# Latent gates merged in one bank per feature tile, and score masks issued behind all of a head's products

## The chip, the cores and the metric

The kernel runs on one core of a Trainium2 chip. The metric is the device time of one execution in microseconds (us), the median over repeated executions. The profile is one such execution, recorded by the hardware; all times are in us from its first instruction unless marked ns.

## The reference

Two networks run one after the other on one sequence of 256 tokens with 2048 features, all in float32. The first has four layers, of three kinds; the change touches two of the kinds.

```python
# layers 0 and 3: differential attention, 8 heads, two score maps a head
sc = einsum('bqhcd,bkhcd->bhcqk', q[:, s:e], k[:, :e]) * scale
sc = where(chunk_mask(s, e - s, e), sc, -inf)
pr = softmax(sc)
w = pr[:, :, 0] - lam * pr[:, :, 1]
# layer 1: latent attention, 16 heads
c_q, c_kv, k_pe, gate = split(xn @ w_in, ...)
sc = (einsum('bqhd,bkhd->bhqk', q_nope, k_nope) + einsum('bqhr,bkr->bhqk', q_pe, k_pe)) * scale
sc = where(chunk_mask(s, e - s, e), sc, -inf)
y = einsum('bhqk,bkhe->bqhe', softmax(sc), v) * silu(gate)
```

A query sees all keys of its own 64-token chunk and of those before it. Queries are taken 128 at a time, the first block with 128 keys, the second with 256. Layer 2 is a gated linear recurrence. After each of the four a gated projection of a side input is added. The second network has one state-space layer and one dilated attention layer. Neither is touched by the change.

## The kernel before

**Products in three parts.** Float32 weights and activations are each split into a high part and a rest, and a product is hi·hi + hi·lo + lo·hi. `chunks` (L307) walks over the feature blocks of 128 (k), loads the weights on SyncE's queue 1 MB at a time (`load`, L285: three buffers), and splits them (`split`, L291) 1024 columns at a time: the high part by ScalarE (L300), the rest by VectorE (L302), three buffers each. After each block it calls `ktick`, and after each chunk `chunk_tick`.

**Order of work.** TensorE's order is mostly the program's. The main line is the large projections. Everything else of a head (norms, rotations, scores, softmax, weighted sums) is written as a job, a generator that yields a number of ticks to wait; `ktick` (L261) steps jobs whose wait is over, so their instructions fall between the products of a projection. Loads and splits get a higher priority, 150 instructions ahead. A planner orders each engine's instructions by priority and by readiness and gives out the buffers.

**Two forms of the product with features on partitions.** `matB` (L326) issues three products of 256 columns for each block and feature tile: hi with the activations' high part, hi with their rest, lo with their high part (L335), all into the same 256 columns of a PSUM bank. `matM` (L349) is the merged form: hi with high part and rest side by side, 512 columns (L357), then lo with the high part, 256 columns (L358); the two halves of the result are added afterwards by `join` (L361): ScalarE copies one half out (L364) and VectorE adds it to the other (L365). `matA` (L374, products on L385) has tokens on partitions.

**Differential attention** (`layer_a`, L782). For each of four groups of two heads the key, query, gate and value projections run, then two `head` jobs (L851). A head (L855 to L881) takes for each of the two query blocks t and each of the two maps c a float32 score product (L861; TensorE runs a float32 product as two instructions), then a mask product in bfloat16 (L864): a matrix whose first row is minus a large number for the first 64 queries, times ones, 64 columns wide. VectorE takes the maximum (L867), GpSimd scales it (L869), ScalarE takes exponentials and sums (L873). After a wait come the transposes (L888 to L890), and later the weighted sum (L895 to L897).

**Latent attention** (`layer_b`, L967). First the latents (`latents`, L1030, by `matM`), then the 64 shared key features. Then gates and head pairs alternate, eight of each (L1211): `gate(q)` (L1182) projects 256 features of the output gate by `matB` into one bank, multiplies by the token norm (L1189) and applies SiLU (L1191); `heads(m)` (L1204) projects queries and keys and values of two heads by `matA` and starts the jobs `uq` (L1066; squares on L1074, transposes L1062 and L1097), `ukv` (L1100; squares L1112, scaled keys L1051, transposes L1062, copied out by L1064) and, 11 ticks later, `pair` (L1123). So the jobs of pair m run within the gate that follows it, and the rest of `pair` (the scaling L1156, the transposes L1164, the sums L1173 to L1178) within the next projections. `pair` takes for each query block two float32 products over 128 features (L1133), two over the 64 rotated features (L1137, on half the rows of the array each) and two masks (L1140).

**PSUM.** Small results share four banks (`ps`, L241); the large accumulators have two of two banks each.

Of the kernel before, what the change touches and what calls it, by code (L numbers as in the profile page):

```python
# [13 lines left out]
BF16 = mybir.dt.bfloat16  # L14
# [4 lines left out]
P = 128  # L19
T = 256  # L20
# [29 lines left out]
for _n, _c in _ROW_SPEC:  # L50
# [6 lines left out]
    "a_w_out": (16, [512] * 4, None),  # L57
    "b_w_in": (16, [256] * 4 + [64] + [256] * 8, None),
    "b_w_uq": (4, [384] * 8, None),
# [129 lines left out]
class Build:  # L189
# [116 lines left out]

    def chunks(self, W, kts, n0, n, merged=False):  # L307

# [4 lines left out]
        for k0, k1 in zip(cuts[:-1], cuts[1:]):  # L313
            src = W.part(n0, n, k0, k1)
            with self.tc.high_priority(offset=self.ahead):
                if self.early:
                    self.early.pop(0)()
                w = self.load(src, k1 - k0, n)
                parts = self.split(w, k1 - k0, n)
            for k in range(k0, k1):  # L320
                yield k, parts[k - k0]
                if not merged or k % 2:
                    self.ktick()
            self.chunk_tick()
# [24 lines left out]
    def matM(self, W, kts, n0, x):  # L349

        a = self.pa.tile([P, 2, 512], F32, name="acc", tag="acc")
        for k, (hi, lo) in self.chunks(W, kts, n0, 256, True):
            xh, _ = x(k)
# [148 lines left out]
    def setup(self):  # L502
# [34 lines left out]
        nc.vector.memset(self.mask[0:1, 0:64], -BIG)  # L537
        self.ones16 = cp.tile([P, 64], BF16, name="ones16")
        nc.vector.memset(self.ones16, 1.0)
# [242 lines left out]
    def layer_a(self, layer, j, x, acc, prep):  # L782
# [68 lines left out]
        def head(h, pend, w1, w2):  # L851
            g, c0 = h // 2, 2 * (h % 2)
            self.finish(*pend)
            vs = slice(T * (h % 2), T * (h % 2) + T)
            ws = []  # L855
            for t in range(2):
                nk = (t + 1) * P
                sc = self.ps()
                scv = sc[:, :2 * nk].rearrange("p (c k) -> p c k", c=2)
                for c in range(2):  # L860
                    nc.tensor.matmul(  # L861
                        out=scv[:, c, :], lhsT=Q[g][:, c0 + c, t * P:(t + 1) * P], rhs=K[g][:, c0 + c, :nk],
                        start=True, stop=False)
                    nc.tensor.matmul(  # L864
                        out=scv[:, c, nk - 64:], lhsT=self.mask, rhs=self.ones16, start=False, stop=True)
                mx = self.small([P, 2])
# [100 lines left out]
    def layer_b(self, layer, x, acc, prep):  # L967
# [155 lines left out]
        def pair(m):  # L1123
# [6 lines left out]
            for t, o0, nk in spans:  # L1130
                qs = slice(t * P, (t + 1) * P)
                for i in range(2):
                    nc.tensor.matmul(  # L1133
                        out=scs[i][:, o0:o0 + nk], lhsT=QT[g][:, c + i, qs], rhs=KT[g][:, c + i, :nk], start=True, stop=False)
                for i in range(2):
                    pr = slice(64 * i, 64 * i + 64)
                    nc.tensor.matmul(  # L1137
                        out=scs[i][:, o0:o0 + nk], lhsT=QPv[pr, qs], rhs=st["kpe"][pr, :nk], start=False, stop=False)
                for i in range(2):
                    nc.tensor.matmul(  # L1140
                        out=scs[i][:, o0 + nk - 64:o0 + nk], lhsT=self.mask, rhs=self.ones16, start=False, stop=True)
            mx, nm, sm, rs = (self.small([P, 2, 2]) for _ in range(4))
# [39 lines left out]
        def gate(q):  # L1182

            a = self.ps()
            self.matB(W, 16, 1088 + 256 * q, 256, x, [(a[:, :T], True, False), (a[:, T:], False, True)])
            if q % 2 == 0:
                sg[q // 2] = self.slot()
            t = sg[q // 2][:, 2 * (q % 2):2 * (q % 2) + 2, :]
            nc.vector.tensor_tensor(  # L1189
                out=t, in0=a.rearrange("p (a b) -> p a b", a=2), in1=nst["rb"].unsqueeze(1).to_broadcast([P, 2, T]), op=ALU.mult)  # L1190
            nc.scalar.activation(t, t, AF.Silu)  # L1191

# [802 lines left out]
```

## Time and profile before

| | |
|---|---|
| median of 3 runs | 3326.06 us (3325.78 to 3326.6) |
| the profiled execution | 3327.28 us |
| its span, first to last instruction | 3325.5 us |
| TensorE, busy | 3281.4 us |
| weight loads, busy (beside products) | 2778.0 us |
| VectorE, busy | 2349.4 us |
| ScalarE, busy | 1876.1 us |
| GpSimd, busy | 282.3 us |
| HBM | 206 GB/s over the span |
| granted TensorE clock, mean | 0.995 of full speed |

PE is TensorE's products, PEld its weight loads, DVE VectorE, ACT ScalarE, POOL GpSimd, SP SyncE. A row of the order of time gives start, duration, engine, line, operation, out<-in with shapes, the count of instructions that it merges and, in brackets, the idle time before it and what ended it. Products overlap: the duration of one runs well past the start of the next, so what a product costs is read from starts. `ps` and `acc` are tiles in PSUM, `t` is a temporary, `s` a large slot, `w` raw weights, `hi` and `lo` their split parts.

### The profile page before, as it was taken

Reading aid. Unit: us, or ns where it says so; the run is one execution under the profiler, and the core shown is the slowest. Engines: PE = TensorE matmul, PEld = TensorE weight load, DVE = VectorE, ACT = ScalarE, POOL = GpSimd, SP = SyncE. Lnnn points to the kernel's source line nnn. Section 1 sums busy time; section 2 is a strip of 40 time slices with the busy share of each in tenths; the row PEclk is TensorE's granted clock in tenths of the full one; section 3 lists DMA queues with packets and bytes.
Section 4 is the critical chain, followed back from the end, with each engine's and each line's share of the span. In section 5 each row is a group of like instructions: output and inputs, shape, how many; then the busy total and the mean of one; then the engine's idle time right before and its main releaser. Section 6 shows DMA issues by size and latency. Waiting matters only on the chain. (4 is left out here: it accounts for less than half of the span.)

```text
span 3325.5 us, 45091 instructions
## 1 busy us (share of the span) xinstructions
PE 3281.4 (99%) x17244; PEld 2778.0 (84%) x17244; DVE 2349.4 (71%) x3217; ACT 1876.1 (56%) x2668; POOL 282.3 (8%) x551
## 2 busy tenths in 40 slices
PE   8999999999999999999999999999999999999997
PEld 7888888898888888888888888888888887888887
DVE  8766766666667886776676677777777767787567
ACT  5555545566655776555555554568777545444454
POOL 3111200122100000001112000000000000000002
PEclk9999999999999999999999999999999999999999
DMA  7656666544466545666566565554555666876442
GB/s 276 231 203 222 214 221 225 195 143 143 149 237 222 196 178 196 230 230 223 201 217 213 197 234 204 184 201 166 190 184 184 235 236 238 299 296 240 161 143 102
DMA packets 114345, 686.65 MB, mean 206 GB/s; under 512 B 13328, under 2 KB 14032, under 8 KB 47696
## 3 DMA queue, kind: packets, MB, share of 16 engines
q1 hardware_dynamic: 109152, 670.49, 56.9%
q10 hardware_dynamic: 4976, 13.27, 1.4%
q8 instruction: 135, 2.21, 0.3%
q14 instruction: 82, 0.67, 0.1%
HBM read 681.55 MB, written 2.16 MB: 206 GB/s over the span
## 5 line engine op out<-in xcount | busy, mean ns | idle before, releaser
L300 ACT ACTIVATE hi<-w 128x1024 fp32r<-128x1024 f32 x1082 | 1141.9, 1056 | 1224.0 <-PE acc L385 747.7
L302 DVE TENSOR_TENSOR lo<-w,hi 128x1024 fp32r<-128x1024 f32 x1082 | 1322.0, 1224 | 671.1 <-ACT hi L300 656.5
L357 PE MATMUL acc<-x,hi 128*128 128x512 f32 x2816 | 1003.6, 400 | 2.2 <-ACT t L364 1.5
L385 PE MATMUL acc<-hi,x 128*128 128x512 f32 x2688 | 844.5, 394 | 4.6 <-ACT hi L300 3.2
L385 PE MATMUL acc<-hi,s 128*128 128x512 f32 (+1 forms) x2560 | 791.0, 390 | 2.5 <-DVE t L1085 2.5
L358 PE MATMUL acc<-x,lo 128*128 128x256 f32 x2816 | 790.6, 281 | 0.0
L357 PEld LDWEIGHTS acc<-x,hi 128*128 128x128 f32 x2816 | 528.7, 188 | 130.7 <-issue 5.3
L385 PEld LDWEIGHTS acc<-hi,x 128*128 128x128 f32 x2688 | 502.6, 189 | 109.3 <-ACT hi L300 3.4
L385 PEld LDWEIGHTS acc<-hi,s 128*128 128x128 f32 x2560 | 474.6, 188 | 94.1 <-issue 2.7
L358 PEld LDWEIGHTS acc<-x,lo 128*128 128x128 f32 x2816 | 531.9, 189 | 3.0 <-issue 2.4
L385 PE MATMUL acc<-lo,x 128*128 128x512 f32 x1344 | 527.1, 392 | 5.5 <-DVE lo L302 5.5
L385 PE MATMUL acc<-lo,s 128*128 128x512 f32 (+1 forms) x1280 | 495.7, 387 | 1.7 <-DVE lo L302 1.7
L385 PEld LDWEIGHTS acc<-lo,x 128*128 128x128 f32 x1344 | 253.6, 189 | 60.2 <-DVE lo L302 6.4
L385 PEld LDWEIGHTS acc<-lo,s 128*128 128x128 f32 x1280 | 240.3, 188 | 50.6 <-DVE lo L302 2.9
L1381 DVE SCALAR_TENSOR_TENSOR aacc<-aw,siluc,aacc 128x512 f32<-128x512 f32 x255 | 190.9, 749 | 68.8 <-DMA aw<-in_ada_w_dram 66.0
L335 PE MATMUL ps<-x,hi 128*128 128x256 f32 (+1 forms) x576 | 108.2, 286 | 0.0
L463 POOL TENSOR_TENSOR m<-m,mhalf 128x4 f32<-128x4 f32 (+2 forms) x61 | 80.0, 1311 | 173.1 <-DVE m L1794 164.5
L335 PEld LDWEIGHTS ps<-x,hi 128*128 128x128 f32 (+1 forms) x576 | 88.6, 185 | 1.2 <-DVE x L733 0.2
L1381 DVE SCALAR_TENSOR_TENSOR ssacc<-s,siluc,ssacc 128x512 f32<-128x512 f32 x105 | 78.6, 748 | 9.7 <-DMA s<-in_ada_w_dram 8.5
L1245 DVE SCALAR_TENSOR_TENSOR s<-s,vecs 128x254 f32<-128x254 f32 (+2 forms) x192 | 80.8, 477 | 1.5 <-ACT s L1243 1.3
L335 PE MATMUL ps<-x,lo 128*128 128x256 f32 (+1 forms) x288 | 81.2, 282 | 0.0
L470 POOL TENSOR_TENSOR m<-ss 128x4 f32<-128x4 f32 x7 | 3.2, 461 | 848.0 <-ACT t L695 848.0
(391 smaller groups left out, 2869.5 us busy)
## 6 DMA issues: line engine op xcount, KB each, us to landing
w<-in_a_w_in_dram SPq DMA_DIRECT2D x127, 1024.0 KB, 4.9
w<-in_a_in_w_dram SPq DMA_DIRECT2D x80, 1024.0 KB, 4.8
aw<-in_ada_w_dram SPq DMA_DIRECT2D x136, 512.0 KB, 4.1
w<-in_ple_w_gate_dram SPq DMA_DIRECT2D x64, 1024.0 KB, 5.2
w<-in_kv_w_dram SPq DMA_DIRECT2D x48, 1024.0 KB, 4.8
w<-in_a_w_out_dram SPq DMA_DIRECT2D x32, 1024.0 KB, 5.1
w<-in_c_w_in_dram SPq DMA_DIRECT2D x32, 1024.0 KB, 4.9
w<-in_a_out_w_dram SPq DMA_DIRECT2D x32, 1024.0 KB, 4.9
```

The lines of the kernel that those rows point to most:

```text
L300: nc.scalar.activation(hi[:, :m], src, AF.Copy)
L302: nc.vector.tensor_tensor(out=lo[:, :m], in0=src, in1=hi[:, :m].bitcast(F32), op=ALU.subtract)
L335: self.nc.tensor.matmul(out=o, lhsT=a[:, c0:c1], rhs=b, start=(k == 0 and p == 0 and first), stop=(k == kts - 1 and p == 2 and last))
L357: self.nc.tensor.matmul(out=a[:, i, :], lhsT=hi[:, c], rhs=xx, start=(k == 0), stop=False)
L358: self.nc.tensor.matmul(out=a[:, i, :T], lhsT=lo[:, c], rhs=xh, start=False, stop=(k == kts - 1))
L385: self.nc.tensor.matmul(out=outs[t][:, :n], lhsT=b[:, s], rhs=w, start=(k == 0 and p == 0), stop=(k == kts - 1 and p == 2))
L463: self.nc.gpsimd.tensor_tensor(out=out, in0=in_, in1=h, op=ALU.pow)
L470: self.nc.gpsimd.tensor_tensor(out=q, in0=acc[:, 0:2, :], in1=acc[:, 2:4, :], op=ALU.add)
L1245: nc.vector.scalar_tensor_tensor(out=dst[:, s:], in0=src[:, :T - s], scalar=self.vec(wname, (3 - s) * nct + ct), in1=dst[:, s:], op0=ALU.m ...
L1381: nc.vector.scalar_tensor_tensor(out=st["acc"], in0=w[:, i, :], scalar=c, in1=st["acc"], op0=ALU.mult, op1=ALU.add)
```

## The change

The gate projection takes one feature tile of 128 at a time, in the merged form of two products, each tile into a bank of `ps` of its own; ScalarE copies the second half of the bank out, VectorE adds it to the first half, and multiply and SiLU follow in SBUF once for both tiles. The weights of the gate columns are stored 128 wide for that, one chunk for each tile. `chunks` takes the number of blocks after which it ticks in place of the flag. In a differential head all score products are issued first, then one mask for each query block over both maps (2 x 64 columns). In a latent pair all products over 128 features come first, then those over 64, then one mask for each head over both query blocks. The first product in a bank alone carries the start flag.

```diff
--- before.py
+++ after.py
@@ -55,7 +55,7 @@
 _WEIGHTS = {
     "a_w_in": (16, [512] * 16, None),
     "a_w_out": (16, [512] * 4, None),
-    "b_w_in": (16, [256] * 4 + [64] + [256] * 8, None),
+    "b_w_in": (16, [256] * 4 + [64] + [128] * 16, None),
     "b_w_uq": (4, [384] * 8, None),
     "b_w_ukv": (4, [512] * 8, None),
     "b_w_out": (16, [512] * 4, None),
@@ -304,7 +304,7 @@
                 parts.append((hi[:, k * n:(k + 1) * n], lo[:, k * n:(k + 1) * n]))
         return parts
 
-    def chunks(self, W, kts, n0, n, merged=False):
+    def chunks(self, W, kts, n0, n, every=1):
 
         step = max(1, 2048 // n)
         cuts = list(range(0, kts, step)) + [kts]
@@ -319,7 +319,7 @@
                 parts = self.split(w, k1 - k0, n)
             for k in range(k0, k1):
                 yield k, parts[k - k0]
-                if not merged or k % 2:
+                if k % every == every - 1:
                     self.ktick()
             self.chunk_tick()
 
@@ -349,7 +349,7 @@
     def matM(self, W, kts, n0, x):
 
         a = self.pa.tile([P, 2, 512], F32, name="acc", tag="acc")
-        for k, (hi, lo) in self.chunks(W, kts, n0, 256, True):
+        for k, (hi, lo) in self.chunks(W, kts, n0, 256, 2):
             xh, _ = x(k)
             xx = x.pair(k)
             for i in range(2):
@@ -535,7 +535,7 @@
         self.mask = cp.tile([P, P], BF16, name="mask")
         nc.vector.memset(self.mask, 0.0)
         nc.vector.memset(self.mask[0:1, 0:64], -BIG)
-        self.ones16 = cp.tile([P, 64], BF16, name="ones16")
+        self.ones16 = cp.tile([P, 2, 64], BF16, name="ones16")
         nc.vector.memset(self.ones16, 1.0)
         self.pos = cp.tile([P, 2], F32, name="posf")
         self.posi = posi
@@ -852,17 +852,20 @@
             g, c0 = h // 2, 2 * (h % 2)
             self.finish(*pend)
             vs = slice(T * (h % 2), T * (h % 2) + T)
-            ws = []
+            ws, scs = [], []
             for t in range(2):
                 nk = (t + 1) * P
-                sc = self.ps()
-                scv = sc[:, :2 * nk].rearrange("p (c k) -> p c k", c=2)
+                scv = self.ps()[:, :2 * nk].rearrange("p (c k) -> p c k", c=2)
                 for c in range(2):
                     nc.tensor.matmul(
                         out=scv[:, c, :], lhsT=Q[g][:, c0 + c, t * P:(t + 1) * P], rhs=K[g][:, c0 + c, :nk],
-                        start=True, stop=False)
-                    nc.tensor.matmul(
-                        out=scv[:, c, nk - 64:], lhsT=self.mask, rhs=self.ones16, start=False, stop=True)
+                        start=(c == 0), stop=False)
+                scs.append(scv)
+            for t in range(2):
+                nk = (t + 1) * P
+                nc.tensor.matmul(out=scs[t][:, :, nk - 64:], lhsT=self.mask, rhs=self.ones16, start=False, stop=True)
+            for t in range(2):
+                nk, scv = (t + 1) * P, scs[t]
                 mx = self.small([P, 2])
                 nc.vector.tensor_reduce(out=mx, in_=scv, axis=AX.X, op=ALU.max)
                 nm = self.small([P, 2])
@@ -1131,14 +1134,18 @@
                 qs = slice(t * P, (t + 1) * P)
                 for i in range(2):
                     nc.tensor.matmul(
-                        out=scs[i][:, o0:o0 + nk], lhsT=QT[g][:, c + i, qs], rhs=KT[g][:, c + i, :nk], start=True, stop=False)
+                        out=scs[i][:, o0:o0 + nk], lhsT=QT[g][:, c + i, qs], rhs=KT[g][:, c + i, :nk],
+                        start=(t == 0), stop=False)
+            for t, o0, nk in spans:
+                qs = slice(t * P, (t + 1) * P)
                 for i in range(2):
                     pr = slice(64 * i, 64 * i + 64)
                     nc.tensor.matmul(
                         out=scs[i][:, o0:o0 + nk], lhsT=QPv[pr, qs], rhs=st["kpe"][pr, :nk], start=False, stop=False)
-                for i in range(2):
-                    nc.tensor.matmul(
-                        out=scs[i][:, o0 + nk - 64:o0 + nk], lhsT=self.mask, rhs=self.ones16, start=False, stop=True)
+            for i in range(2):
+                nc.tensor.matmul(
+                    out=scs[i].rearrange("p (a k) -> p a k", a=2)[:, :, 64:P], lhsT=self.mask, rhs=self.ones16,
+                    start=False, stop=True)
             mx, nm, sm, rs = (self.small([P, 2, 2]) for _ in range(4))
             es = [self.tmp(384), self.tmp(384)]
             for i in range(2):
@@ -1181,14 +1188,20 @@
 
         def gate(q):
 
-            a = self.ps()
-            self.matB(W, 16, 1088 + 256 * q, 256, x, [(a[:, :T], True, False), (a[:, T:], False, True)])
             if q % 2 == 0:
                 sg[q // 2] = self.slot()
-            t = sg[q // 2][:, 2 * (q % 2):2 * (q % 2) + 2, :]
-            nc.vector.tensor_tensor(
-                out=t, in0=a.rearrange("p (a b) -> p a b", a=2), in1=nst["rb"].unsqueeze(1).to_broadcast([P, 2, T]), op=ALU.mult)
-            nc.scalar.activation(t, t, AF.Silu)
+            v = sg[q // 2][:, 2 * (q % 2):2 * (q % 2) + 2, :]
+            for i in range(2):
+                a = self.ps()
+                for k, (hi, lo) in self.chunks(W, 16, 1088 + 256 * q + P * i, P, 2):
+                    xh, _ = x(k)
+                    nc.tensor.matmul(out=a, lhsT=hi, rhs=x.pair(k), start=(k == 0), stop=False)
+                    nc.tensor.matmul(out=a[:, :T], lhsT=lo, rhs=xh, start=False, stop=(k == 15))
+                u = self.tmp(T)
+                nc.scalar.activation(u, a[:, T:], AF.Copy)
+                nc.vector.tensor_tensor(out=v[:, i, :], in0=a[:, :T], in1=u, op=ALU.add)
+            nc.vector.tensor_tensor(out=v, in0=v, in1=nst["rb"].unsqueeze(1).to_broadcast([P, 2, T]), op=ALU.mult)
+            nc.scalar.activation(v, v, AF.Silu)
 
         def close(j):
             self.finish(pairs[2 * j], pairs[2 * j + 1])
```

## Rows read from the trace of the kernel before

**Rows 1.** The page's first part: TensorE's products, busy us, share, instructions.

```profile
PE 3281.4 (99%) x17244; PEld 2778.0 (84%) x17244; DVE 2349.4 (71%) x3217; ACT 1876.1 (56%) x2668; POOL 282.3 (8%) x551
```

**Rows 2.** Busy time by stretch: length, PE, PEld, DVE, ACT, POOL, clock, DMA, GB/s.

```profile
100.00:410.00 310.00, 309.83 (x1451) 256.02 (x1450) 213.02 (x281) 168.19 (x256) 54.63 (x123) 1.00 0.61 215
...
705.25:733.17 27.92, 27.77 (x193) 25.06 (x192) 17.73 (x38) 17.68 (x32) 7.16 (x16) 1.00 0.41 142
718.49:728.99 10.50, 10.50 (x67) 9.66 (x66) 7.33 (x15) 10.24 (x19) 0.20 (x1) 1.00 0.54 184
```

**Rows 3.** Order of time, TensorE, ten triples of a gate apart.

```profile
677.79 0.40 PE L335 MATMUL ps<-x,hi 128*128 128x256 f32 x2
...
681.39 0.40 PE L335 MATMUL ps<-x,hi 128*128 128x256 f32 x2
```

**Rows 4.** Order of time, TensorE, 18 merged pairs of the latents apart.

```profile
629.82 0.39 PE L357 MATMUL acc<-x,hi 128*128 128x512 f32 x1
...
636.06 0.39 PE L357 MATMUL acc<-x,hi 128*128 128x512 f32 x1
```

**Rows 5.** Order of time, VectorE, within one period of layer 1.

```profile
712.83 0.76 DVE L1051 TENSOR_TENSOR t<-acc,m 128x256 f32<-128x256 f32 x2 [1.97 <-POOL m L625]
713.50 2.08 DVE L302 TENSOR_TENSOR lo<-w,hi 128x1024 fp32r<-128x1024 f32 x2
...
721.49 0.69 DVE L1189 TENSOR_TENSOR s<-ps,rb 128x512 f32<-128x512 f32 x1 [1.16 <-PE ps L335]
...
725.69 0.55 DVE L1156 TENSOR_SCALAR t<-t,m 128x128 f32<-128x128 f32 x2
```

**Rows 6.** Groups of 650 to 870: count, busy us, mean ns, idle before.

```profile
L1112 ACT ACTIVATE t<-acc 128x256 f32<-128x256 f32 x14 | 5.4, 385 | 14.4 <-PE ps L335 13.5 <-DVE t L612 0.9
```

**Rows 7.** Waits of weight loads, 650 to 910: total us, times, longest.

```profile
PEld ps L1164 <- PE acc L385: 2.0, 8, 0.4
PEld ps L1062 <- issue: 1.9, 6, 0.3
```

**Rows 8.** Order of time, TensorE: the key heads' transposes.

```profile
713.40 0.68 PE L1062 MATMUL ps<-ident,t 128*128 128x128 f32 x4
```

**Rows 9.** Order of time, ScalarE: first and last of the full stretch.

```profile
718.49 0.84 ACT L300 ACTIVATE hi<-w 128x768 fp32r<-128x768 f32 x1 [3.68 <-PE ps L335]
...
728.06 0.87 ACT L1074 ACTIVATE t<-acc 128x384 f32<-128x384 f32 x2
```

**Rows 10.** Order of time, TensorE: scores and masks of a differential head.

```profile
112.49 0.38 PE L861 MATMUL ps<-s 128*128 128x128 f32 x2
112.71 0.19 PE L864 MATMUL ps<-ones,mask 128*128 128x64 bf16 x1
112.73 0.47 PE L861 MATMUL ps<-s 128*128 128x128 f32 x2
113.04 0.19 PE L864 MATMUL ps<-ones,mask 128*128 128x64 bf16 x1
...
114.15 0.71 PE L385 MATMUL acc<-hi,x 128*128 128x512 f32 x2
```

**Rows 11.** Order of time, TensorE: scores and masks of a latent pair.

```profile
686.94 0.71 PE L1133 MATMUL ps<-s 128*128 128x128 f32 x4
687.58 0.49 PE L1137 MATMUL ps<-s 64*128 64x128 f32 x4
688.01 0.23 PE L1140 MATMUL ps<-ones,mask 128*128 128x64 bf16 x2
688.07 1.11 PE L1133 MATMUL ps<-s 128*128 128x256 f32 x4
689.11 0.70 PE L1137 MATMUL ps<-s 64*128 64x256 f32 x4
689.75 0.23 PE L1140 MATMUL ps<-ones,mask 128*128 128x64 bf16 x2
689.82 0.37 PE L335 MATMUL ps<-x,hi 128*128 128x256 f32 x1
```

## The prediction

> **What bounds the kernel now.** I began with the busy shares. TensorE is busy for 99% of the span [rows 1], so only time on its own instruction stream can be saved, and an added instruction elsewhere matters only where TensorE ends up waiting for it. The profiled execution took 3327.28 us, its span is 3325.5, and the median of the three runs is 3326.06; the sum below is a difference and is taken off the median.
>
> Next came the busy time by stretch [rows 2]. In the first attention layer TensorE is busy for 309.83 of 310.00 us: nothing is waited for there, and what its stream loses the kernel gains. One period of the latent layer, a gate and a head pair's projections, is 27.92 us long, and seven of the eight gates are followed by one. The other engines look free in it, at 17.7 us each. But one stretch of 10.50 us within the period has ScalarE busy for 10.24. That is where the argument turns.
>
> Last I read the order of time of each engine around the three places that the diff edits [rows 3 to 11].
>
> **Gates, on TensorE.** A gate has 16 feature blocks times 2 halves. Each now takes three products of 256 columns; with the change it takes one of 512 and one of 256. The columns are equal, and one weight load and one start in three go. Ten such triples take 681.39 − 677.79 = 3.60 us, 0.360 each [rows 3]. The merged form already stands in this layer's latents: 18 pairs take 636.06 − 629.82 = 6.24 us, 0.3467 each [rows 4]. The difference is 0.0133 us, times 32 it is 0.43 us a gate, times 8 gates 3.4 us, if all of it reached the end.
>
> Weight transfers stay: one load of 1 MB per half replaces one of 1 MB per 8 blocks, 8 KB a partition both times, as many splits, and the background ticks come after the same number of columns. SyncE gets nothing new.
>
> **Gates, on the other engines.** One VectorE multiply out of PSUM of 512 columns (0.69 us, at 721.49 [rows 5]) becomes two ScalarE copies and two VectorE adds of 256 columns out of PSUM, and the same multiply within SBUF. The nearest ScalarE row is 385 ns, an instruction of the same shape out of PSUM [rows 6]; behind another it may cost less, so I take 0.28 to 0.385. The nearest VectorE row is 0.76 for two [rows 5], 0.38 each.
>
> **What the gates' gain meets.** In six of the eight gates TensorE waits 0.3 us ahead of the transposes of the key heads [rows 7]: their inputs are two VectorE instructions begun at 712.83 and together 0.76 long, and TensorE starts on the first of them at 713.40 [rows 5, 8]. VectorE itself had waited 1.97 us for GpSimd. That chain through ScalarE, VectorE and GpSimd begins where the row of 718.49 begins it for the next period: TensorE frees a buffer of split weights right behind the score products. From there ScalarE runs nearly without a gap up to the squares of the query projection at 728.06 [rows 2, 9], and everything after hangs on those. So the period is the length of this chain plus the score products, and TensorE's faster gates only lengthen its wait. Of the 32 triples only one or two, between the score products and the freed buffer, still shorten the period: 0.02 us.
>
> The copy of a gate's second half falls into that full ScalarE stretch (the multiply that follows the gate starts at 721.49 [rows 5]), so the chain grows by 0.28 or more. The copy of the first half is ready near 711.6 (the gate's start at 705.25 [rows 2], 16 pairs of 0.347 and six transposes at the 0.11 of a small product), where VectorE idles until 712.83 [rows 5]; I cost it at nothing. What hides it is that idle stretch, and if its order is bad it holds up the transposes by the add's 0.38.
>
> **Masks of the differential heads.** A head now issues eight score products, with a mask of 64 columns after every two. Two small products alone take 112.71 − 112.49 = 0.22 us; behind a mask they take 113.04 − 112.73 = 0.31 [rows 10]. A mask streams for 0.03 and is too short to cover the load of the next float32 weights: about 0.085 is exposed behind each of the four, the last one ahead of the next projection. With the change all eight products stand first, and two masks of 128 columns follow. Their columns are equal, three of four exposures go, and the last shrinks by the 0.03 that the longer mask covers, to 0.055. A head saves 4 × 0.085 − 0.055 = 0.28 us; 2 layers of 8 heads save 4.5 us.
>
> The first query tile's maximum now waits for the second tile's products: at 112.49 + 4 × 0.11 + 4 × 0.216 = 113.79 its mask starts, 0.75 later than the one at 113.04. VectorE's queue behind that maximum holds the next split of weights, and TensorE needs that only two or three buffers later, so I cost it at nothing. The second tile is 0.25 earlier, and the transposes wait for it. Bounds: 0.2 to 0.34 a head.
>
> **Masks of the latent pairs.** A pair takes 689.82 − 686.94 = 2.88 us from its first score product to the gate's next product [rows 11], and eight pairs run. By its rows: the change from 128-row to 64-row products costs about 0.09 (0.64 for four products of 0.11, of which 0.10 is the first weight load) and comes once instead of twice; the exposure behind the middle masks, 0.085, goes; four masks of 0.03 to 0.04 become two of 0.056, saving 0.02; the last exposure shrinks by 0.03. Sum 0.23 us a pair, 1.8 us in all.
>
> Four 64-row products over 128 columns take 688.01 − 687.58 = 0.43 us, two groups of 0.21, so about 0.10 a group is lost even between two groups of the same kind [rows 11]; I keep that loss. The Trainium skill's page "TensorEngine Tiling (Array Packing)", Key Properties, says that changing the tiling mode drains the engine and changing only the tile does not. By that the two groups that become neighbours would lose nothing, and a pair would save 0.33 instead of 0.23.
>
> **The sum.** Heads −4.5. The first gate, which meets no key chain, −0.4. The second, with most of its triples ahead of waits, −0.2. The first and the last pair, which lie outside the steady periods, −0.5. In each of seven periods −0.23 (pair) − 0.02 (triples) + 0.28 (copy) + 0.10 (the add and the longer chain on VectorE, taken low because only part of it stands in the way) = +0.13, so +0.9. Total −4.7 us, taken against 3326.06: 3321.4 us, and 3322.6 for a profiled execution like the one shown.
>
> About 0.2%, 6.65 us, is what a measurement of this kernel can tell from no change. The forecast lies inside it.
>
> **Rivals.** *The full gain.* If the order of ScalarE's queue comes out so that no copy stands in the chain, or the splits run further ahead because a chunk has fewer instructions, the terms are 3.4 + 4.5 + 1.8 = 9.7 us: 3316.4. For it: VectorE and ScalarE are free 10 us in each period [rows 2]. Against it: the six waits of 0.3 us, which stand before any copy is added. Chance 0.25.
>
> *The add and the multiply land before the softmax's last scaling.* VectorE scales the second head's weights at 725.69 [rows 5], and TensorE already waits in all eight pairs for its transposes [rows 7]. An add of 0.38 and a multiply of 0.69, less overlap, are 0.94 us in that queue; the periods then lose 0.94 − 0.25 = 0.69 each, 4.8 in all, and −5.6 + 4.8 = −0.8: 3325.3. It decides from about 0.8 us a period. Chance 0.13.
>
> *A bank is held (slower).* A gate now fills two banks of the four that it shares with the transposes and scores. If the first half's add stands behind the two splits of 713.50 (2.08 us [rows 5]) its bank comes free at 713.50 + 2.08 + 0.38 = 715.96, and a score product due one period after 686.94 [rows 11], at 714.86, waits 1.1 us. Over seven periods that is 7.7: 3329.1. Beyond 0.67 us a period the gain of 4.7 is gone. Against it: the key transposes' own bank is free again by then. Chance 0.08.
>
> *Masks over two separate runs stream slower.* Both new masks write two runs of 64 columns; no row shows such a product. If it took twice its 0.056, 48 masks would add 2.7 us: 3324.1. The Trainium skill's "PSUM — Partial Sum Buffer", Specifications (TRN2), warns that any non-contiguous access pattern slows matmuls significantly, by no stated figure; no row here bears that out. Chance 0.05.
>
> **How the numbers follow.** The forecast has 0.49. Faster by over 0.2% is the full gain and the forecast's good edge, 0.29. Slower by over 0.2% needs waits for a bank of 1.6 us a period, or two of the costs at once: 0.07. The rest, 0.64, is within. The range runs from the full gain with the heads at their upper bound (3.4 + 16 × 0.34 + 1.8 = 10.6: 3315.4) to the second rival with the masks' price on top (3325.3 + 2.7 = 3328.0), and leaves out the held bank.
>
> **What would show it.** In the changed profile a gate pair of products should start every 0.347 us; a head should span 1.41 us from its first product to the next projection instead of 1.66; a pair 2.68 instead of 2.88. The period should stay between 27.8 and 28.2 us, with the wait ahead of the key transposes grown to 0.5 us or more and ScalarE's stretch longer by one copy. The forecast is wrong if the period falls below 27.5 (the chain did not bind) or rises past 28.5 (another wait), or if heads span over 1.5 us.

## The result, and the profile after

The changed kernel takes 3345.33 us (median of 4 runs, 3344.52 to 3346.83) against 3326.33 for the kernel before; the ratio is 1.0055, with a 95% interval of 1.0043 to 1.0066. It is 19 us slower, and the prediction's range ended at 3328.0. The profiled execution took 3345.09 us, its span is 3343.0.

The page's first part, with the engines' busy time, answers to [rows 1]:

```profile
PE 3277.3 (98%) x16940; PEld 2761.5 (83%) x16940; DVE 2353.9 (70%) x3233; ACT 1880.9 (56%) x2684; POOL 274.7 (8%) x551
```

TensorE has 4.1 us less to do in 304 fewer instructions, VectorE and ScalarE have 4.5 and 4.8 us more. None of this is 19 us: nearly all of the time was lost in waits. The busy time by stretch answers to [rows 2] (same columns); the second line is one period of the latent layer, from a query projection to the next:

```profile
100.00:410.00 310.00, 309.73 (x1442) 255.81 (x1441) 214.39 (x284) 169.13 (x257) 55.72 (x123) 1.00 0.61 217
754.05:784.48 30.43, 27.46 (x161) 23.12 (x160) 18.56 (x39) 18.34 (x33) 6.49 (x15) 1.00 0.37 130
```

The first attention layer is as full as before. The period has grown from 27.92 to 30.43 us, and TensorE is idle for 2.97 us of it, at a granted clock of 1.00. From the first query projection to the second there are +1.8 us, in each of the six periods behind it +2.5, behind the last projection +3.6 (14.71 to 18.26) and in the layer's last stretch +1.3: 21.8 us. The first layer gives back 1.7, later heads and the rest 2.6.

The +1.3 is no wait. Behind the last projection TensorE stands idle for 2.05 and then for 3.46 us, and the output projection that follows runs at a granted clock of 0.50, the 1.2 GHz level: nine products in 3.97 us. The kernel before is idle there for 2.46 us, keeps a clock of 1.00 and takes 2.15. The first two rows are the changed kernel's first and tenth product, the last two those of the kernel before:

```profile
894.16 1.19 PE L385 MATMUL acc<-hi,s 128*128 128x512 f32 x2 [3.46 <-DVE t L1088]
...
898.13 0.71 PE L385 MATMUL acc<-hi,s 128*128 128x512 f32 x2
```

```profile
875.65 0.70 PE L385 MATMUL acc<-hi,s 128*128 128x512 f32 x2 [2.46 <-DVE t L1085]
...
877.80 0.61 PE L385 MATMUL acc<-hi,s 128*128 128x512 f32 x2
```

So 1.8 us of the loss is clock, behind a longer wait; the rest of that stretch is 0.5 shorter than before.

What the edits did on TensorE itself is seen in the order of time: a differential head and the projection behind it, a latent pair and the gate product behind it, and two products of a gate ten pairs apart. These answer to [rows 10], [rows 11] and [rows 3].

```profile
113.04 1.47 PE L860 MATMUL ps<-s 128*128 128x128 f32 x8
114.35 0.27 PE L866 MATMUL ps<-ones,mask 128*128 128x128 bf16 x2
114.43 0.47 PE L385 MATMUL acc<-hi,x 128*128 128x512 f32 x1
...
687.37 1.58 PE L1136 MATMUL ps<-s 128*128 128x128 f32 x8
688.88 0.93 PE L1143 MATMUL ps<-s 64*128 64x128 f32 x8
689.73 0.29 PE L1146 MATMUL ps<-ones,mask 128*128 128x128 bf16 x2
689.83 0.36 PE L1199 MATMUL ps<-x,lo 128*128 128x256 f32 x1
...
705.43 0.40 PE L1198 MATMUL ps<-x,hi 128*128 128x512 f32 x1
...
708.96 0.40 PE L1198 MATMUL ps<-x,hi 128*128 128x512 f32 x1
```

A head takes 114.43 − 113.04 = 1.39 us (1.66 before), a pair 689.83 − 687.37 = 2.46 (2.88 before), a gate's pair of products 3.53 / 10 = 0.353 (0.360 before). All three edits made TensorE's own work shorter.

The waits of TensorE in the latent layer, 650 to 930 us, answer to [rows 7] (total us, times, longest). The products' own waits and those of their weight loads overlap, so the lines aren't added:

```profile
PE ps L1100 <- DVE t L613: 12.1, 14, 1.2
PE ps L1065 <- DVE t L1054: 8.8, 7, 2.0
...
PEld ps L1100 <- DVE t L613: 14.2, 13, 1.5
PEld ps L1065 <- issue: 10.9, 7, 2.4
```

Before, the longest wait that comes back in every period was 0.4 us. Now the rotary transposes of the queries (L1100) and the transposes of the query and key heads (L1065) come late in every period, behind VectorE's rotary sums (L613) and head scalings (L1054), which wait for GpSimd's norms: the chain that starts with the squares of the query projection. ScalarE's order of time shows why these are late. First the kernel before; the query projection starts at 749.21:

```profile
751.38 1.06 ACT L300 ACTIVATE hi<-w 128x1024 fp32r<-128x1024 f32 x1
752.46 1.28 ACT L1191 ACT_TABLE_LOAD   x1
753.75 0.63 ACT L1191 ACTIVATE s<-s 128x512 f32<-128x512 f32 x1
754.29 1.04 ACT L300 ACTIVATE hi<-w 128x1024 fp32r<-128x1024 f32 x1
755.24 0.86 ACT L1166 ACTIVATE t<-ps 128x384 f32<-128x384 f32 x2
755.98 0.87 ACT L1074 ACTIVATE t<-acc 128x384 f32<-128x384 f32 x2
```

Then the changed kernel, where the projection starts at 754.03:

```profile
756.37 1.06 ACT L300 ACTIVATE hi<-w 128x1024 fp32r<-128x1024 f32 x1
757.32 0.39 ACT L1201 ACTIVATE t<-ps 128x256 f32<-128x256 f32 x1
757.89 0.88 ACT L1173 ACTIVATE t<-ps 128x384 f32<-128x384 f32 x2 [0.19 <-PE ps L1171]
759.14 1.06 ACT L300 ACTIVATE hi<-w 128x1024 fp32r<-128x1024 f32 x1 [0.37 <-PE acc L385]
760.11 0.48 ACT L1077 ACTIVATE t<-acc 128x384 f32<-128x384 f32 x1
760.60 1.28 ACT L1204 ACT_TABLE_LOAD   x1
761.89 0.63 ACT L1204 ACTIVATE s<-s 128x512 f32<-128x512 f32 x1
762.43 1.04 ACT L300 ACTIVATE hi<-w 128x1024 fp32r<-128x1024 f32 x1
763.38 0.47 ACT L1077 ACTIVATE t<-acc 128x384 f32<-128x384 f32 x1
```

Before, SiLU and its table load (752.46) stand ahead of the two squares (755.98), and the squares end 7.64 us after the projection's start. Now SiLU waits for the copy (757.32), and behind that for an add and a multiply on VectorE:

```profile
758.79 0.42 DVE L1202 TENSOR_TENSOR s<-ps,t 128x256 f32<-128x256 f32 x1
759.24 0.69 DVE L1203 TENSOR_TENSOR s<-s,rb 128x512 f32<-128x512 f32 x1
```

ScalarE goes on with other work meanwhile: both weight transposes (L1173), one more weight copy (759.14), one square (760.11). Then SiLU with its load comes between the two squares, a weight copy behind it, and the second square ends at 763.85, 9.82 us after the start, 2.18 later. By the rows, the second square has one more weight copy ahead of it (0.97 from start to start), the eviction's copy with the idle time behind it (757.32 to 757.89, 0.57) and another idle 0.37: 1.9 of the 2.18 us.

### The profile page after: what moved, and what is told of

Same layout as the page of the kernel before. It is cut to its first block, busy times and chain, and to the rows that moved or that the text cites. A ratio compares the mean times of both kernels' runs of the same rounds, so it can differ in the third digit from the quotient of the medians.

```text
span 3343.0 us, 44520 instructions
## 1 busy us (share of the span) xinstructions
PE 3277.3 (98%) x16940; PEld 2761.5 (83%) x16940; DVE 2353.9 (70%) x3233; ACT 1880.9 (56%) x2684; POOL 274.7 (8%) x551
## 5 line engine op out<-in xcount | busy, mean ns | idle before, releaser
L1198 PE MATMUL ps<-x,hi 128*128 128x512 f32 x256 | 94.0, 406 | 0.0
L463 POOL TENSOR_TENSOR m<-m,mhalf 128x4 f32<-128x4 f32 (+2 forms) x61 | 73.0, 1197 | 173.1 <-DVE m L1807 164.5
L1199 PE MATMUL ps<-x,lo 128*128 128x256 f32 x256 | 72.9, 285 | 0.0
L365 DVE TENSOR_TENSOR s<-acc,t 128x512 f32<-128x512 f32 x88 | 60.2, 684 | 2.2 <-ACT t L364 2.1
```

Of the source, the lines that this page charges most:

```text
L365: self.nc.vector.tensor_tensor(out=out, in0=a[:, :, :T], in1=u, op=ALU.add)
L463: self.nc.gpsimd.tensor_tensor(out=out, in0=in_, in1=h, op=ALU.pow)
L1198: nc.tensor.matmul(out=a, lhsT=hi, rhs=x.pair(k), start=(k == 0), stop=False)
L1199: nc.tensor.matmul(out=a[:, :T], lhsT=lo, rhs=xh, start=False, stop=(k == 15))
```

## The experiments

Each theory's claim stands in the expectations. In short: **T1**, SiLU's new place on ScalarE; **T2**, the regrouped masks hold score banks; **T4**, the eviction as such, with **T4b**, the gate's bank held until VectorE's add; **T5**, temporaries; **T6**, the merged products. For every kernel the table has the median, the ratio to the kernel before with its 95% interval, the mean of five periods (from the first product of one query projection to that of the next), and the end of the second square after the projection's start in one period (for the first two kernels the one that the rows above show).

```
kernel                            us      ratio, interval           period  2nd square
before                            3326.3  1                         27.93   7.64
the change                        3345.3  1.0055 (1.0043 to 1.0066) 30.46   9.82
gate only                         3350.4  1.0073 (1.0059 to 1.0087) 30.89   9.81
masks only                        3318.6  0.9970 (0.9958 to 0.9981) 27.57   7.64
pair masks only                   3322.6  0.9990 (0.9981 to 0.9998) 27.50   7.64
SiLU later                        3327.4  0.9998 (0.9989 to 1.0007) 28.31   6.92
before, SiLU later                3326.3  0.9996 (0.9987 to 1.0004) 27.92   7.64
one multiply, no copy and add     3318.2  0.9975 (0.9965 to 0.9984) 27.57   7.80
SiLU later, no temporary          3327.1  1.0005 (0.9996 to 1.0013) 28.29   6.93
SiLU later, whole bank copied     3322.2  0.9990 (0.9981 to 0.9999) 27.34   6.93
old products, long eviction       3325.6  0.9997 (0.9988 to 1.0006) 27.80   6.88
the same, SiLU between squares    3344.6  1.0055 (1.0042 to 1.0067) 30.12   9.79
whole bank copied, SiLU not later 3344.5  1.0054 (1.0041 to 1.0068) 30.36   9.82
first gate old, others improved   3320.2  0.9978 (0.9969 to 0.9987) 27.33   6.93
```

The kernel before moved by up to 1.6 us between the sessions (3326.33 to 3327.97), so times of different sessions are compared by their ratios.

**Gate only, masks only, pair masks only.** The change's diff with other hunks taken back; against the changed kernel, the heads' and pairs' masks in the first, the gate in the second, gate and heads in the third:

```
-                        start=(c == 0), stop=False)
-                scs.append(scv)
...
+                        start=True, stop=False)
+                    nc.tensor.matmul(
+                        out=scv[:, c, nk - 64:], lhsT=self.mask, rhs=self.ones16[:, 0, :], start=False, stop=True)
```

```
-    "b_w_in": (16, [256] * 4 + [64] + [128] * 16, None),
+    "b_w_in": (16, [256] * 4 + [64] + [256] * 8, None),
...
+            a = self.ps()
+            self.matB(W, 16, 1088 + 256 * q, 256, x, [(a[:, :T], True, False), (a[:, T:], False, True)])
```

> The gate's part of the change alone, both mask edits undone. Theory T1 (the gate's new copy, add and multiply make SiLU late, so that SiLU with its table load stands between the two squares of the next query projection on ScalarE and the period of the second layer grows by 2.5 us): the gate brings the whole loss and more, since the masks gave some back; 3349 to 3353 us, period of the gates 30.4 us. Rival T2 (the regrouped masks of the latent pairs hold the score banks longer and cost the period): 3326 to 3330, period near 28. Rival T3 (both together): in between.

> The two mask edits alone, the gate as before. T1: faster than before by what the change has gained by the end of the first layer (1.8 to 2.3 us) and by about as much again in the later heads and in the pairs: 3319 to 3323 us, period 27.7 to 27.9. T2: slower than before, up to 3345. The sum of this run's difference and of the gate's alone, each against before, should be the change's +19 us if the two parts do not act on each other.

> The mask edit of the latent pairs alone. 0.23 us a pair by the working of the prediction, 7 or 8 pairs: 1.6 to 1.9 us less than before, 3324 to 3325 us; the rest of what the masks gave together (some 9 us below before) is then of the heads, whose score products the edit regroups 16 times in each of two layers. If TensorE is not the bound of the period: no change, 3326 to 3328.

The gate is the whole loss: +22.4 us, the masks −9.4, the pairs' masks alone −3.9 (−1.6 to −1.9 was expected). T2 is out. The parts add up only roughly: 22.4 − 9.4 = +13.0, where the change has +19.0. Alone, the pairs' masks shorten the period by 0.43, all that they save on TensorE (2.88 − 2.46), and within the change (30.89 to 30.46) by the same 0.43. The masks of the heads thus have some 5 us, against 16 × 0.27 = 4.3 by the head's rows; the intervals are ±4 us wide. The 6 us by which the sum is off are no more than the three intervals (±4.7, ±3.8 and ±3.8 us) leave open together (about ±7, the root of the sum of their squares): of the period nothing is missing, and the other layers differ by a few microseconds from one profile to the next.

**SiLU later.** In the changed kernel, and in the kernel before.

```
-            nc.scalar.activation(v, v, AF.Silu)
+            sj[q] = self.go(silu(v), 6)
...
-            self.finish(pairs[2 * j], pairs[2 * j + 1])
+            self.finish(pairs[2 * j], pairs[2 * j + 1], sj[2 * j], sj[2 * j + 1])
```

> The change whole, with SiLU alone put off by six ticks of TensorE's work, so that ScalarE's order has both squares of the query projection ahead of SiLU and its table load; the copies, the adds and the multiplies stay. T1: the squares come up to 2.9 us earlier (1.28 + 0.63 of SiLU and 1.04 of the copy behind it), the period falls from 30.4 to 27.5 to 28.0, and the time to 3320 to 3328 us. Rival T4 (the cost lies in the eviction itself: the temporaries taken, the VectorE work added, the banks held): no change, 3343 to 3347.

> The kernel before with the same deferral of SiLU. If the period of the kernel before is set by ScalarE's chain through the query squares, taking 1.9 us of SiLU out from ahead of them shortens it until TensorE's own work is the bound: the waits in a period are some 0.6 us, so 0.3 to 0.6 us by 7 periods, 3321 to 3324 us. If the chain ends elsewhere (keys, softmax), no change: 3325.5 to 3327.5; and if SiLU then stands ahead of the key squares and these are the later ones, slower: up to 3335.

Moving SiLU alone takes 18 us off the change (19 by the ratios), and the squares end at 6.92 instead of 9.82. In the kernel before the same edit left ScalarE's order as it was (SiLU still ahead of the squares, which end at 7.64 as ever), so that run decides nothing about what bound the period there.

3327.4 still isn't 3320. The order of time of this kernel shows a wait that the changed kernel has not, between the first and the second score product of a pair (two instructions each):

```profile
742.37 0.36 ACT L1206 ACTIVATE t<-ps 128x256 f32<-128x256 f32 x1
...
743.46 2.08 DVE L302 TENSOR_TENSOR lo<-w,hi 128x1024 fp32r<-128x1024 f32 x2
...
745.47 0.41 DVE L1207 TENSOR_TENSOR s<-ps,t 128x256 f32<-128x256 f32 x1
...
746.03 0.35 PE L1136 MATMUL ps<-s 128*128 128x128 f32 x1 [0.72 <-DVE s L1207]
```

The first half's bank was copied at 742.37, but VectorE adds from it only behind two weight splits, and a score product waits for the bank. Three runs bear on this:

**One multiply a bank, no copy and add; no temporary; whole bank copied.**

```
-                u = self.tmp(T)
-                nc.scalar.activation(u, a[:, T:], AF.Copy)
-                nc.vector.tensor_tensor(out=v[:, i, :], in0=a[:, :T], in1=u, op=ALU.add)
-            nc.vector.tensor_tensor(out=v, in0=v, in1=nst["rb"]..., op=ALU.mult)
+                nc.vector.tensor_tensor(out=v[:, i, :], in0=a[:, :T], in1=nst["rb"], op=ALU.mult)
```

```
+                nc.scalar.activation(v[:, i, :], a[:, T:], AF.Copy)
+                nc.vector.tensor_tensor(out=v[:, i, :], in0=a[:, :T], in1=v[:, i, :], op=ALU.add)
```

```
+                u = self.tmp()
+                nc.scalar.activation(u, a, AF.Copy)
+                nc.vector.tensor_tensor(out=v[:, i, :], in0=u[:, :T], in1=u[:, T:], op=ALU.add)
```

> The change with its gate products as they are, but each bank emptied by one VectorE multiply of its first half (256 elements): the copies, the adds and the second half of each bank are left out, so ScalarE has SiLU ahead of both query squares again as in the kernel before. T1 (the loss is SiLU's lateness behind copy, add and multiply): the loss is gone, and TensorE's saving of 0.43 us a gate stands beside the masks' gain: 3315 to 3320 us. T4b (the gate now takes two score banks a period where it took one, and the score pair waits for the first of them): a wait of the pair's products of some 0.7 us a period stays, 3321 to 3326.

> The change with SiLU put off by six ticks, as in the run before, and the copy written into the gate's own tile instead of a temporary. T5 (what stays of the loss are temporaries that come free late): 1 us less in a period, 3318 to 3321. T4b (the bank is held until VectorE's add, the temporaries are idle): no change against the deferral alone, 3325 to 3329.

> The change with SiLU put off by six ticks, and the whole bank (512 elements) copied out by ScalarE, so that the bank is free with the copy and not with VectorE's add, which stands behind two weight splits of 2.08 us. The copy becomes 0.2 us longer. T4b: the wait of the pair's products on the add (0.72 us a period) goes, the period falls from 28.3 to 27.6 or less: 3319 to 3323 us. T5, or a wait that is only moved: 3325 to 3329.

With no copy and no add in front of it, SiLU runs ahead of the squares again and the loss is gone (3318.2). But the period is 27.57, as with the masks alone: the merged products bring nothing. Without the temporary nothing changes (28.29), so T5 is out. With the whole bank copied the period falls by 0.97 to 27.34, and the score product no longer waits, for the bank is empty after the copy at 738.88 and VectorE's add, still behind its splits, reads the copy:

```profile
738.88 0.58 ACT L1206 ACTIVATE t<-ps 128x512 f32<-128x512 f32 x1
...
741.29 1.58 PE L1136 MATMUL ps<-s 128*128 128x128 f32 x8
741.94 0.42 DVE L1207 TENSOR_TENSOR s<-t 128x256 f32<-128x256 f32 x1
```

T4b holds, for 0.97 us a period of the kernel with SiLU put off. That is 0.25 more than the wait of 0.72 that goes; where the rest comes from I did not trace.

**SiLU's place alone.** The next two kernels have the masks of the change, the gate's old products in one bank and a long eviction; they differ in what fixes SiLU's place. First the eviction of both, then what the second adds, which makes SiLU write where the second square writes next:

```
+            u = self.tmp(T)
+            nc.scalar.activation(u, a[:, T:], AF.Copy)
+            for i in range(2):
+                nc.vector.tensor_tensor(out=t[:, i, :], in0=a[:, :T], in1=u, op=ALU.add)
+            nc.vector.tensor_tensor(out=t, in0=t, in1=nst["rb"]..., op=ALU.mult)
```

```
                 sq = self.tmp(384) if t == 0 else None
+                if t == 1:
+                    sq = self.tmp()
+                    nc.scalar.activation(sq.rearrange("p (a b) -> p a b", a=2), late.pop(), AF.Silu)
+                    sq = sq[:, :384]
                 nc.scalar.activation(sq, a[:, t, :384], AF.Square)
```

> The mask edits with the gate's old products in one bank, but emptied through a copy of 256 elements on ScalarE, two adds and one multiply on VectorE (the values are not the gate's: the copied half is added to the first half twice). ScalarE's order has SiLU behind both query squares here. T1 (what costs is SiLU's place on ScalarE, not the eviction's work): near the mask edits alone, 3318 to 3324 us. T4 (the eviction's added work itself costs): 3328 or more.

> The same kernel with one thing changed: SiLU writes into the scratch tile of the second query square, so that it must stand between the two squares as in the changed kernel (its result is lost, and the gate goes on without SiLU). Same products, same eviction, same instructions. T1: the second square ends some 2.2 us later after the start of the query projection, the period grows by 2 to 2.6 us over the run with SiLU behind the squares: 3336 to 3346 us. T6 (the loss needs the merged products or their two banks): no change against that run.

ScalarE's order in the first of them (the projection starts at 748.48), then in the second (753.60):

```profile
754.48 0.87 ACT L1077 ACTIVATE t<-acc 128x384 f32<-128x384 f32 x2
755.37 1.28 ACT L1201 ACT_TABLE_LOAD   x1
```

```profile
759.64 0.48 ACT L1083 ACTIVATE t<-acc 128x384 f32<-128x384 f32 x1
760.14 1.28 ACT L1081 ACT_TABLE_LOAD   x1
761.44 0.63 ACT L1081 ACTIVATE t<-s 128x512 f32<-128x512 f32 x1
761.97 1.04 ACT L300 ACTIVATE hi<-w 128x1024 fp32r<-128x1024 f32 x1
762.92 0.47 ACT L1083 ACTIVATE t<-acc 128x384 f32<-128x384 f32 x1
```

Same products, same instructions, one order changed: 19 us. The square comes 2.9 us later, where the changed kernel has it (9.79 against 9.82), and the period lands near it (30.12 against 30.46). T6 is out, T1 is shown. But the first run shows also the price of the long eviction itself. Its 3325.6 lies above T1's 3318 to 3324, between the theories, and 7 us above the masks alone (9 by the ratios, ±5). The rows place about 4 of these: 2.7 from the first query projection to the second (28.15 against 25.43), and 0.23 in each of six periods (27.80 against 27.57). So of the 27 to 28 us that lie between the masks alone and the change, SiLU's place has 19, and T4 has most of the rest.

**Whole bank copied, SiLU not later**, and a version from the findings: the first gate with its old products and eviction, the other seven merged, copied out whole, SiLU six ticks later:

```
-    "b_w_in": (16, [256] * 4 + [64] + [128] * 16, None),
+    "b_w_in": (16, [256] * 4 + [64] + [256] + [128] * 14, None),
...
+            if q == 0:
+                a = self.ps()
+                self.matB(W, 16, 1088, 256, x, [(a[:, :T], True, False), (a[:, T:], False, True)])
...
+                return
```

> The change with the whole bank (512 elements) copied out by ScalarE, and SiLU not put off: ScalarE's order has SiLU ahead of both squares, but behind copy, add and multiply. The bank is free as early as in the run with copy and deferral (3322 us). T1: the squares are as late as in the changed kernel, both of them now behind SiLU: 3336 to 3348 us. If the bank were the main loss: 3320 to 3325.

> A version from the findings: masks as in the change, the first gate with its old products and eviction (the changed kernels lose about 2 us ahead of the second gate), the other seven merged, copied out whole by ScalarE and with SiLU put off by six ticks. By the run with copy and deferral (3322 us) less those 2 us: 3318 to 3321 us, about level with the mask edits alone (3318.6); if the loss at the first gate only moves to the second, 3322.

Emptying the bank early brings next to nothing while the squares are late (30.36 against 30.46): here both squares stand behind SiLU, and the second ends at 9.82 all the same. So the bank's wait was hidden under the late squares. The last version is 0.22% faster than the kernel before, and the mask edits alone are 0.30% faster: the intervals overlap, and the mask edits are the smaller change, so they are the version to keep.

From the change to that version the time falls in three steps, by the ratios: SiLU's place 19 us (1.0055 to 0.9998), the held bank 3 to 5 (0.9998 and 1.0005 to 0.9990), the first gate 4 (to 0.9978). Each step has ±4 to 5 us, so the two small ones rest on the rows: 0.97 us a period for the bank, and for the first gate the stretch ahead of the second projection. From the first query projection to the second, every kernel with the long eviction at the first gate takes 27.7 to 28.2 us, the others 25.2 to 25.8.

## Why the prediction was wrong

**Where the time hangs: right.** "Everything after hangs on those" squares, the prediction said of ScalarE's full stretch. That is what happened, and a period past 28.5 was the sign that it had named for another wait: with the second square at 9.8 us the period is 30.1 to 30.9 in four kernels, at 6.9 to 7.8 it is 27.3 to 28.3 in ten. That the period was nothing but this chain is not borne out: with the square 0.7 us earlier than in the masks alone, the old products' period is not shorter but longer (27.80).

**The step that failed is the term of the copy**, "the chain grows by 0.28 or more". It priced the copy as one more instruction in an unchanged order. But SiLU, which had hung on one multiply, now hung on copy, add and multiply, and lost its place ahead of the squares. The term measured 2.18 us at the square, and the +0.13 a period of the sum came out as +2.5. Outside the periods the sum had −1.1 for the first two gates and the first and last pair; the rows have −0.3 ahead of the first query projection, +1.8 behind it, and +3.6 and +1.3 at the layer's end. I had read the stretch's ends [rows 9] and its fill [rows 2], not the rows between, where SiLU and its load, 1.9 us, stand ahead of the squares and hang on the multiply that the change puts behind a copy and an add. The rest of the 2.9 us that the gate costs in a period (30.46 against 27.57) lies behind the square: from its end to the key transposes are 13.4 us (763.85 to 777.22) where the kernel before takes 12.4 (two periods behind [rows 8] the transposes start at 769.26, the square ends at 756.85). Nearly all of it lies ahead of the first key square, which comes 7.23 us behind the second query square in the kernel before and 8.14 in the changed one:

```profile
764.08 0.39 ACT L1112 ACTIVATE t<-acc 128x256 f32<-128x256 f32 x1 [1.94 <-PE ps L335]
```

```profile
771.99 0.38 ACT L1115 ACTIVATE t<-acc 128x256 f32<-128x256 f32 x1 [2.08 <-DVE t L613]
```

There it waits for a rotary sum of the queries (L613), and among VectorE's rotary instructions stands a weight split of 1.48 us (769.94). What puts it there I did not test.

**Gates on TensorE: oversized.** The ten pairs shown take 0.353 us each; over all 205 undisturbed pairs of the eight gates the mean is 0.351, and 0.359 for the triples before, not 0.347 and 0.360 as read from two short stretches [rows 3, 4]. So a gate saves 0.27 us instead of 0.43, 2.1 in all; the first gate, which meets no wait, shows just that (63.84 to 63.57 us from the first latent product to the first query projection). Even with no copy and add the other gates' savings didn't come through (27.57 both ways): as forecast, TensorE then waits for the key transposes instead, 3.0 us over six periods where the masks alone have 0.3.

**Heads: right.** 1.39 us against 1.41 forecast.

**Pairs: undersized.** 0.42 us against 0.23, and all of it reached the period. What the sum had is there: the exposure behind the middle masks (by the single starts 299 − 216 = 83 ns), one change to 64 rows (205 − 112 = 93) and the shorter masks (135 − 95 = 40). What it had kept as a loss goes too. The two 64-row groups that become neighbours lose their 0.1 us each: the second 128-column group now lasts 105 ns instead of 205, the first 256-column group 212 instead of 313. These 0.20 are the whole difference. The group that still precedes a change keeps its 308. I had read the loss as one of every 64-row group. The rule of the Trainium skill's "TensorEngine Tiling (Array Packing)", Key Properties, that changing the mode drains the engine and changing the tile does not, agrees with this trace; by it I had 0.33, which counts 0.10 for the two groups where the rows give 0.20, and 0.43 would have been the sum.

**The rivals.** *Add and multiply ahead of the softmax's last scaling*: no, that scaling begins at 756.73 in the changed kernel, the add at 758.79. *A held bank*: the mechanism is there, as described, behind the two splits of 2.08 us; the wait is 0.72 us where 1.1 was forecast, and it is worth 0.97 a period, but only once SiLU is out of the way, so it didn't decide. *Masks over two runs stream slower*: no. By the single starts the first mask of a pair takes 67 ns for its two runs, where one run of 64 columns took 38, and the first mask of a head 55 where one run took 28: no more for a column. (The last mask ahead of another product takes 28 or 29 at either width and tells nothing.) The warning of "PSUM — Partial Sum Buffer", Specifications (TRN2), in the Trainium skill isn't borne out for two runs of 64 columns. *The full gain*: no; the gates had 2.1 of their 3.4 us to give, and the squares came later.

## What to carry to other kernels

Before an eviction is lengthened, list what waits for its last instruction and where that stands in its engine's order; an instruction that misses its slot on a full engine costs what is scheduled into the slot and what it then pushes back, here 2.18 us at the square where a copy of 0.39 had been added. A late instruction that nobody needs soon, as SiLU here, is worth putting off explicitly behind the work that others wait for. And two faults can hide each other: only with the first mended did the held bank show.

## What was not expected of the hardware

A merged pair of 512 and 256 columns has no one time: single pairs take 0.340 to 0.361 us, with a mean of 0.351 in the gates and 0.347 in the latents, the weights loaded and the activations streaming in both; I have no cause for it. A mask of two separate runs of 64 columns in a bank is no slower for a column than one run (55 ns against 28). And where 64-row products follow each other, the loss of 0.1 us stands only at the group next to a change of mode. A wait can cost a second time: behind waits of 2.05 and 3.46 us TensorE's clock was at its 1.2 GHz level for the next nine products, and the three other kernels with the late square show that level there too. Which wait brings it these runs don't tell: the kernel before kept 2.4 GHz behind one of 2.46 us, the masks alone lost it for some products behind one of 2.27.
